# Half of gate_a moved from TensorE to VectorE, with four smaller edits, in a one-core hybrid mLSTM layer step

## The chip, the cores and the metric

The kernel runs on one core of one Trainium2 chip. The metric is device microseconds (us) of one execution, inputs in the chip's main memory at the start and outputs there at the end. Everything is single precision; the large products are done as three matmuls each on rounded parts (high by high, high by low, low by high), written "hi" and "lo" in the code.

## The reference, cut to what matters

```python
mod = silu(c) @ ada_w + ada_b            # (2048) @ (2048, 6*2048), for c_ctx and for c
shift_a, scale_a, gate_a, shift_f, scale_f, gate_f = mod split in 6
h = rmsnorm(x, norm_w[0]) * (1 + scale_a) + shift_a
q, k, v, o, gates, u = split(h @ w_in)   # 1024, 1024, 1024, 1024, 32, 1024 columns
hm = mlstm_bidirectional(q, k, v, gates, states)
hm = rmsnorm(hm) * sigmoid(o)
hp = pool_mixer(u)
mix = concat(hm, hp) @ w_out             # (T, 2048) @ (2048, 2048)
x = x + gate_a * rmsnorm(mix, norm_w[1])
h = rmsnorm(x, norm_w[2]) * (1 + scale_f) + shift_f
y = square(relu(h @ w1)) @ w2            # 2048 -> 8192 -> 2048
x = x + gate_f * rmsnorm(y, norm_w[3])
```

There are 384 tokens: 128 of a context (modulated by `c_ctx`) and 256 latent ones (modulated by `c`); `GROUPS` in the kernel are these two ranges of columns. The outputs are `x` and the final mLSTM states of the context.

## The kernel before, in words

Activations lie transposed, features on the 128 partitions and the 384 tokens along the free axis, in tiles of `[128, 386]` (`slot`). A weight tile of `[128, 1024]` (512 KB) is loaded by the SP queue (`load_w`, L118), rounded to its high part by ScalarE (L124), and its low part is made by VectorE (L125). There are three raw buffers and four of each part. `gemm_T` takes such tiles in order: per tile 24 matmuls (8 times `mm3`, L133 to L135), and after each tile it calls the *feeds*: generators that each advance by `rate` steps a call (`Feed`), so that side work is written between the matmuls of the main work. A scheduler then orders each engine's queue from the order in the program, by its own estimate of what is ready when.

Stages: **u and v** (to about 209 us; eight steps of two 128-row blocks, five weight chunks each, with the matvecs for shift_a and scale_a between them by `ADA_STEPS`), **q and k** (209 to 415 us; four pairs of products; the first takes pooling and gates as feeds, the other three take `attention` of the heads before), **o** (to 502 us), **w_out** (502 to 646 us, 32 weight tiles), then the row norm `r1` (`token_rstd_rows`, L771, POOL at L186, L194) and `make_h2` (L823 to L831), then the **MLP**: per 1024 hidden features four `gemm_T` on w1 (128 x 386 columns: 384 tokens and two columns that carry the shift), and `mlp_out` on w2 (L876 to L878, 128 x 512). From 744 us on this repeats eight times. A tail of norm and residual ends it.

The modulation vectors are matvecs over `ada_w`, 512 KB a load (L212 or L250), four buffers under the tag `ada`. They are made in two ways:

- `ada_mat`, on TensorE: per load four matmuls of 256 columns (L216), which the trace shows as eight records, since a single-precision matmul has two; they lie in four column groups of the array. It ends with a copy (L221) and small matmuls (L224).
- `ada_vec`, on VectorE: per load, products with a per-partition scalar added into an accumulator `ada_acc` (L261 the first, L263 the others), here 512 columns wide, two rows of `ada_w` a load and two conditions, so four instructions a load. It ends with four matmuls by ones (L274), a copy (L276) and small transposing matmuls (L280).

Before the change: shift_a and scale_a by `ada_mat` in the u and v stage; gate_a by `ada_mat` (feed `ada1`, 0.75 steps a call); scale_f and shift_f by `ada_vec` in eight blocks of 512 columns (feed `ada2`, 1.32 steps a call); the first quarter of gate_f by `ada_mat`, the rest by `ada_vec`. Of that first quarter's eight loads four are done while `r1` is worked out (`fill`), four between the first w1 matmuls (`first_side`). gate_a scales the output of w_out as it leaves PSUM (L755).

Of the kernel before, what the change touches and what calls it, by code (L numbers as in the profile page):

```python
# [29 lines left out]
N_E = 1  # L30
ADA_STEPS = (3, 3, 3, 0, 0)
X_ORDER = "tatatatabtatatatat"
N_X = 2


@with_exitstack
def hymba_kernel(
# [26 lines left out]
    cc = const.tile([P, 2, 16], F32, name="cc")  # L64
    prm = const.tile([P, 2, P], F32, name="prm")
# [134 lines left out]

    def ada_mat(parts, tags=("ada",)):


        n, nk = len(parts), parts[0][2]
        w, nj = nk * P, 8 // nk
        ps = bank(f"ada_{parts[0][0]}_{parts[0][1]}")
        for b, (i, k0, _) in enumerate(parts):
            c0 = i * D + k0 * P
            for j0 in range(0, 16, nj):
                tag = tags[b % len(tags)]  # L210
                raw = wp.tile([P, nj, w], F32, tag=tag, name=f"ada_raw_{i}_{k0}_{j0}", bufs=N_W if tag == "lo" else N_ADA)
                nc.sync.dma_start(raw, aw[:, j0:j0 + nj, c0:c0 + w])  # L212
                for a in range(nj):
                    j = j0 + a
                    g = j % 4
                    nc.tensor.matmul(ps[32 * g:32 * g + 32, 0:w], cT[:, j, 6 - 2 * b:38 - 2 * b], raw[:, a, :],  # L216
                                     start=b == 0 and j < 4, stop=b == n - 1 and j >= 12)
# [228 lines left out]
    def gates():  # L446
# [19 lines left out]
        tri = ((C_U, C_NU), (C_L, C_NL))  # L466
        for d in range(2):
            r = slice(32 * d, 32 * d + 8)
            for i in range(3):
                cols = slice(i * P, (i + 1) * P)  # L470
                nc.tensor.matmul(ps_a[r, cols], gv[:, i, d, 0, :], ident, start=True, stop=False)
                nc.tensor.matmul(ps_a[r, cols], lf[:, i, d, :], cst[:, tri[d][1], :], start=False, stop=True)
                nc.tensor.matmul(ps_b[r, cols], lf[:, i, d, :], cst[:, tri[d][0], :], start=True, stop=True)
        for d in range(2):
# [27 lines left out]
        for src, dst in ((aS, acol), (bS, ecol), (gS, gcol)):  # L502
            ps = bank("ps_col")
            i0 = 1 if dst is gcol else 0
            for i in range(i0, 3):
                nc.tensor.matmul(ps[:, i * 40:(i + 1) * 40], src[0:40, i, :], ident[0:40, 0:40], start=True, stop=True)
# [170 lines left out]

# [139 lines left out]
    def make_h2(k):  # L817
# [4 lines left out]
        m = mo[k]  # L822
        nc.vector.tensor_tensor(m[:, 0:NTOK], r1bc[:, 0:NTOK], m[:, 0:NTOK], op=ALU.mult)  # L823
# [245 lines left out]
```

## Time and profile before

| what | value |
|---|---|
| median of 3 runs | 1751.73 us (1749.28 to 1759.74) |
| profiled execution: time, span | 1754.28 us, 1752.6 us |
| busy: TensorE, its weight loads, VectorE, ScalarE, GpSimd | 1716.6, 1537.4, 1065.9, 639.4, 144.3 us |
| mean granted clock of TensorE | 0.996 |
| transfers | 320.74 MB, 183 GB/s over the span |

In the views, PE is TensorE's matmuls, PEld its weight loads, DVE is VectorE, ACT is ScalarE, POOL is GpSimd, and SPq is the SP queue that issues transfers. A matmul is pipelined: its record lasts about 340 ns while the next starts 175 ns later, so what it costs is read from the distance of starts, and not from its duration. `x8` in a row of the timeline is a merged run of eight records.

### The profile page before, as it was taken

How to read it: one execution, taken by the hardware profiler on the slowest of the kernel's cores; microseconds unless marked ns; L12 is line 12 of the kernel's file. 1: busy time of each engine (PE TensorE's matmuls, PEld its weight loads, DVE VectorE, ACT ScalarE, POOL GpSimd, SP SyncE). 2: the span in 40 equal slices, each digit the busy share in tenths (PEclk: the TensorE clock that was granted, in tenths of full speed). 3: DMA queues.
4: the chain of work that ended last, by engine and by line, in shares of the span. 5: the costliest groups of instructions: out<-in, count | busy, mean ns of one | idle time of the engine just before them, and what ended most of it. 6: DMA issues, size and time to landing. Idle time of an engine off the chain costs nothing.

```text
span 1752.6 us, 24767 instructions
## 1 busy us (share of the span) xinstructions
PE 1716.6 (98%) x9617; PEld 1537.4 (88%) x9617; DVE 1065.9 (61%) x1760; ACT 639.4 (36%) x1092; POOL 144.3 (8%) x186
## 2 busy tenths in 40 slices
PE   6999999999999999999999999999999999999997
PEld 3777899998899989988988988988988988998986
DVE  3677658787898849974444843448444444443446
ACT  4322344445433336432332432422332332332332
POOL 0000001111102225430000000000000000000100
PEclk9999999999999999999999999999999999999999
DMA  9888957877777775773434734435444435434543
GB/s 304 276 281 282 304 155 245 250 233 230 237 239 232 237 252 160 201 216 122 129 122 126 219 124 123 130 121 168 130 123 124 129 121 168 131 122 139 170 135 108
DMA packets 249605, 320.74 MB, mean 183 GB/s; under 512 B 14368, under 2 KB 186000, under 8 KB 249104
## 3 DMA queue, kind: packets, MB, share of 16 engines
q1 hardware_dynamic: 242096, 303.61, 55.6%
q0 software_dynamic: 5728, 13.69, 2.8%
q10 hardware_dynamic: 1664, 1.87, 0.3%
q8 instruction: 75, 1.23, 0.3%
q14 instruction: 42, 0.34, 0.1%
HBM read 308.61 MB, written 10.51 MB: 182 GB/s over the span
## 4 chain that ended last, share of the span: by engine, by line
PE 86%; DVE 5%; DMA 5%; issue 2%; POOL 1%; ACT 1%; SPq 1%; ACTq 0%; DVEq 0%; POOLq 0%
PE acc_w L133 10%; PE acc_w L134 10%; PE acc_w L135 10%; PE y L876 10%; PE y L877 10%; PE y L878 10%; DMA ada_raw<-in_ada_w_dram 2%; PE ada L216 2%; DVE ada_acc L263 2%; PE acc_wo L133 1%; PE acc_wo L135 1%; PE acc_wo L134 1%; PE acc_o L133 1%; PE u L390 1%; PE u L389 1%
## 5 line engine op out<-in xcount | busy, mean ns | idle before, releaser
L125 DVE TENSOR_TENSOR lo_w<-raw_w,hi_w 128x1024 fp32r<-128x1024 f32 x256 | 313.9, 1226 | 433.3 <-ACT hi_w L124 433.0
L124 ACT ACTIVATE hi_w<-raw_w 128x1024 fp32r<-128x1024 f32 x256 | 271.5, 1061 | 685.4 <-PE acc_w L134 316.1
L133 PE MATMUL acc_w<-h2h,hi_w 128*128 128x386 f32 x1024 | 347.6, 341 | 2.4 <-ACT h2h L827 2.4
L134 PE MATMUL acc_w<-h2l,hi_w 128*128 128x386 f32 x1024 | 348.3, 340 | 0.0
L135 PE MATMUL acc_w<-h2h,lo_w 128*128 128x386 f32 x1024 | 348.1, 340 | 0.0
L263 DVE SCALAR_TENSOR_TENSOR ada_acc<-ada_raw,sg,ada_acc 128x512 f32<-128x512 f32 x330 | 236.7, 767 | 17.3 <-DMA ada_raw<-in_ada_w_dram 17.3
L133 PEld LDWEIGHTS acc_w<-h2h,hi_w 128*128 128x128 f32 x1024 | 194.5, 190 | 5.0 <-ACT h2h L827 3.0
L134 PEld LDWEIGHTS acc_w<-h2l,hi_w 128*128 128x128 f32 x1024 | 194.2, 190 | 0.8 <-issue 0.4
L135 PEld LDWEIGHTS acc_w<-h2h,lo_w 128*128 128x128 f32 x1024 | 194.0, 189 | 0.1
L216 PE MATMUL ada<-ada_raw,cT 128*32 128x256 f32 x832 | 61.2, 394 | 3.7 <-DMA ada_raw<-in_ada_w_dram 3.6
L900 DVE TENSOR_TENSOR y<-y,y 128x512 f32<-128x512 f32 x81 | 55.9, 692 | 11.7 <-PE y L878 11.3
L124 ACT ACTIVATE hi_wo<-raw_wo 128x1024 fp32r<-128x1024 f32 x32 | 34.1, 1067 | 73.0 <-DMA raw_wo<-in_w_out_dram 43.2
L795 POOL DMA_DIRECT2D gf_dram<-gfT x1 | 0.5, 521 | 698.3 <-DVE gfT L794 698.3
L125 DVE TENSOR_TENSOR lo_wo<-raw_wo,hi_wo 128x1024 fp32r<-128x1024 f32 x32 | 38.8, 1221 | 17.9 <-ACT hi_wo L124 17.9
L389 PE MATMUL v<-hi_v,hh 128*128 128x384 f32 (+1 forms) x144 | 48.5, 337 | 0.0
L867 ACT ACTIVATE z<-z,bz 128x128 f32<-128x128 f32 (+1 forms) x128 | 47.4, 441 | 1.0 <-DVE z L865 0.9
L391 PE MATMUL v<-hi_v,hl 128*128 128x384 f32 (+1 forms) x144 | 46.7, 324 | 0.0
L390 PE MATMUL v<-lo_v,hh 128*128 128x384 f32 (+1 forms) x144 | 46.5, 323 | 0.0
L133 PE MATMUL acc_k<-hh,hi_k 128*128 128x384 f32 x128 | 44.7, 349 | 0.0
L133 PE MATMUL acc_o<-hh,hi_o 128*128 128x384 f32 x128 | 44.6, 348 | 0.0
L133 PE MATMUL acc_q<-hh,hi_q 128*128 128x384 f32 x128 | 44.5, 348 | 0.0
L216 PEld LDWEIGHTS ada<-ada_raw,cT 128*32 128x32 f32 x832 | 19.7, 109 | 27.4 <-issue 14.7
(949 smaller groups left out, 3627.0 us busy)
## 6 DMA issues: line engine op xcount, KB each, us to landing
raw_w<-in_w_dram SPq DMA_DIRECT2D x256, 512.0 KB, 3.7
ada_raw<-in_ada_w_dram SPq DMA_DIRECT2D x192, 512.0 KB, 4.8
raw_wo<-in_w_out_dram SPq DMA_DIRECT2D x32, 512.0 KB, 5.0
raw_u<-in_w_in_dram SPq DMA_DIRECT2D x16, 512.0 KB, 7.5
raw_q<-in_w_in_dram SPq DMA_DIRECT2D x16, 512.0 KB, 5.9
raw_k<-in_w_in_dram SPq DMA_DIRECT2D x16, 512.0 KB, 4.9
raw_o<-in_w_in_dram SPq DMA_DIRECT2D x16, 512.0 KB, 5.0
raw_v<-in_w_in_dram SPq DMA_DIRECT2D x16, 384.0 KB, 7.5
```

What stands on the lines that cost most here:

```text
L124: nc.scalar.activation(hi[:, 0:n], raw[:, 0:n], AF.Copy)
L125: low = lambda: nc.vector.tensor_tensor(lo[:, 0:n], raw[:, 0:n], hi[:, 0:n].bitcast(F32), op=ALU.subtract)
L133: nc.tensor.matmul(ps, lh, rh, start=start, stop=False)
L134: nc.tensor.matmul(ps, lh, rl, start=False, stop=False)
L135: mm3.ins = nc.tensor.matmul(ps, ll, rh, start=False, stop=stop).ins
L216: nc.tensor.matmul(ps[32 * g:32 * g + 32, 0:w], cT[:, j, 6 - 2 * b:38 - 2 * b], raw[:, a, :], start=b == 0 and j < 4, stop=b == n - 1 and ...
L263: nc.vector.scalar_tensor_tensor(acc[:, g, :], raw[:, a, :], cj, acc[:, g, :], op0=ALU.mult, op1=ALU.add)
L389: nc.tensor.matmul(acc[i][:, 0:n], xh[:, sl], hi[:, k, :], start=k == 0, stop=False)
L390: nc.tensor.matmul(acc[i][:, 0:n], xh[:, sl], lo[:, k, :], start=False, stop=False)
L876: nc.tensor.matmul(acc, xh[:, s], hi, start=k == 8 * ch, stop=False)
L877: nc.tensor.matmul(acc, xh[:, s], lo, start=False, stop=False)
L878: nc.tensor.matmul(acc, xl[:, s], hi, start=False, stop=k == 8 * ch + 7)
```

## The change

- gate_a: of its 16 blocks of 128 columns the last eight stay with `ada_mat` (feed `ada1`, now at 0.35 steps a call); the first eight go to `ada_vec`.
- `ada_vec` for scale_f, shift_f and that half of gate_a runs in five blocks of 1024 columns (one row of `ada_w` a load, so two instructions of 1024 columns), at 1.5 steps a call in q and k and 1.3 in o and w_out. `prm` moves from the pool `const` to the pool `pre`.
- gate_a is applied in `make_h2` (a fused scale and multiply per token group, in place of one multiply), and the copy out of PSUM becomes plain.
- All eight `ada_mat` loads of gate_f come in two calls of `fill`, the second behind the broadcast of `r1`; its second four loads go to the still unused output tiles `y[0]`, `y[1]`.
- After the first MLP chunk's w2 product has begun, `norm_h2` multiplies h2 by the second row norm and adds the shift, so that all later w1 products have 384 columns and leave PSUM by `evac_normed`.
- In `gates` the matmuls of the two directions alternate; eight small matmuls by the identity (L506) become transposes.
- `ADA_STEPS` goes from (3, 3, 3, 0, 0) to (4, 0, 4, 1, 0).

```diff
-ADA_STEPS = (3, 3, 3, 0, 0)
+ADA_STEPS = (4, 0, 4, 1, 0)
+RATES = (1.5, 1.3, 1.3)
+RATE_MAT = 0.35
...
-                raw = wp.tile([P, nj, w], F32, tag=tag, ...)
+                if raws and tag is None:
+                    raw = raws.pop(0).rearrange("p (j c) -> p j c", c=w)
+                else:
+                    raw = wp.tile([P, nj, w], F32, tag=tag, ...)
...
-        for d in range(2):
-            r = slice(32 * d, 32 * d + 8)
-            for i in range(3):
-                ...
+        for i in range(3):
+            for part in range(3):
+                for d in range(2):
+                    r = slice(32 * d, 32 * d + 8)
+                    ...
-                nc.tensor.matmul(ps[:, i * 40:(i + 1) * 40], src[0:40, i, :], ident[0:40, 0:40], start=True, stop=True)
+                nc.tensor.transpose(ps[:, i * 40:(i + 1) * 40], src[0:40, i, :], ident[0:40, 0:40])
...
-        for i in (4, 3):
-            for q in range(4):
-                yield from ada_vec(i, 512 * q, 512, att)
-    ada1 = Feed(mid_mat(), 0.75)
-    ada2 = Feed(mid_vec(), 1.32)
+        for i, q in ((4, 0), (4, 1), (3, 0), (3, 1), (2, 0)):
+            yield from ada_vec(i, 1024 * q, 1024, att)
+    ada1 = Feed(ada_mat([(2, 8 + 2 * b, 2) for b in range(4)]), RATE_MAT)
+    ada2 = Feed(mid_vec(), RATES[0])
...
-            for g, (a, b) in enumerate(GROUPS):
-                nc.scalar.activation(m[:, a:b], mo[u][:, a:b], AF.Copy, scale=mod[:, 2, u, g:g + 1])
+            nc.scalar.activation(m[:, 0:NTOK], mo[u][:, 0:NTOK], AF.Copy)
...
+    def norm_h2():
+        for k, (hi, lo) in enumerate(h2):
+            t = mlp.tile([P, NTOK], F32, tag="z", name=f"h2n{k}")
+            nc.vector.tensor_tensor(t, hi[:, 0:NTOK].bitcast(F32), lo[:, 0:NTOK].bitcast(F32), op=ALU.add)
+            nc.vector.tensor_tensor(t, t, r2bc, op=ALU.mult)
+            for g, (a, b) in enumerate(GROUPS):
+                sh = mod[:, 3, k, g:g + 1]
+                nc.scalar.activation(hi[:, a:b], t[:, a:b], AF.Identity, bias=sh)
+                nc.vector.scalar_tensor_tensor(lo[:, a:b], t[:, a:b], sh, hi[:, a:b].bitcast(F32), op0=ALU.add, op1=ALU.subtract)
+            yield
+    def evac_normed(t, ps):
+        z = mlp.tile([P, NTOK], F32, tag="z", name=f"z{t}")
+        nc.scalar.activation(z, ps[:, 0:NTOK], AF.Relu)
+        nc.vector.tensor_tensor(z, z, z, op=ALU.mult)
+        hid[t] = split_T(z, f"hid{t}")
...
-        yield from ada_mat([(5, 0, 2), (5, 2, 2)])
+        yield from ada_mat([(5, 0, 2), (5, 2, 2)], ("ada", None), [y[i][:, 1024 * n:1024 * n + 1024] for i in range(2) for n in range(2)])
...
         r1bc = token_rstd_rows([sqa, sqs[0], sqs[1]], "r1", fill)
+        fill()
...
-        nc.vector.tensor_tensor(m[:, 0:NTOK], r1bc[:, 0:NTOK], m[:, 0:NTOK], op=ALU.mult)
+        for g, (a, b) in enumerate(GROUPS):
+            nc.vector.scalar_tensor_tensor(m[:, a:b], m[:, a:b], mod[:, 2, k, g:g + 1], r1bc[:, a:b], op0=ALU.mult, op1=ALU.mult)
...
+        elif ch < 7:
+            gemm_T(w1, [grp(4 * ch + 4)], hx2, NTOK, evac_normed, (ff, fx), name="w1")
...
+        ws = mlp_out(ch, (ff, fx, fn) if ch == 0 else (ff, fx), done if ch == 7 else None)
+        if ch == 0:
+            fn.finish()
```

In `first_side` three of the four steps of gate_f that stood between the w1 matmuls go, since `fill` has taken the loads.

More of the change, by code (lines that the diff above doesn't have):

```diff
@@ L64, in hymba_kernel @@
     cc = const.tile([P, 2, 16], F32, name="cc")
-    prm = const.tile([P, 2, P], F32, name="prm")
+    vp_scope, pre_scope = ExitStack(), ExitStack()
+    vp = vp_scope.enter_context(tc.tile_pool(name="vp", bufs=1))
+    pre = pre_scope.enter_context(tc.tile_pool(name="pre", bufs=1))
+    prm = pre.tile([P, 2, P], F32, name="prm")
     nc.sync.dma_start(cc[:, 0, :], c_ctx.rearrange("(p j) -> p j", j=16))
@@ L68, in hymba_kernel @@
     nc.sync.dma_start(cst[:, 0:3], cs_src[:, 0:3])
-    vp_scope, pre_scope = ExitStack(), ExitStack()
-    vp = vp_scope.enter_context(tc.tile_pool(name="vp", bufs=1))
     vsb = [vp.tile([P, NH, 129], F32, name=f"v{i}") for i in range(3)]
     gsb = vp.tile([P, 3, 32], F32, name="gsb")
-    pre = pre_scope.enter_context(tc.tile_pool(name="pre", bufs=1))
     x_tok = [pre.tile([P, D], F32, tag=f"x{i}", name=f"xtok{i}") for i in range(3)]
@@ L199, in hymba_kernel, with ada_mat @@
     aw = ada_w.rearrange("(p j) n -> p j n", j=16)
-    def ada_mat(parts, tags=("ada",)):
+    def ada_mat(parts, tags=("ada",), raws=None):
         n, nk = len(parts), parts[0][2]
@@ L210, in ada_mat @@
                 tag = tags[b % len(tags)]
-                raw = wp.tile([P, nj, w], F32, tag=tag, name=f"ada_raw_{i}_{k0}_{j0}", bufs=N_W if tag == "lo" else N_ADA)
+                if raws and tag is None:
+                    raw = raws.pop(0).rearrange("p (j c) -> p j c", c=w)
+                else:
+                    raw = wp.tile([P, nj, w], F32, tag=tag, name=f"ada_raw_{i}_{k0}_{j0}", bufs=N_W if tag == "lo" else N_ADA)
                 nc.sync.dma_start(raw, aw[:, j0:j0 + nj, c0:c0 + w])
@@ L466, in gates @@
         tri = ((C_U, C_NU), (C_L, C_NL))
-        for d in range(2):
-            r = slice(32 * d, 32 * d + 8)
-            for i in range(3):
[L470 to L473, printed above, removed]
+        for i in range(3):
+            cols = slice(i * P, (i + 1) * P)
+            for part in range(3):
+                for d in range(2):
+                    r = slice(32 * d, 32 * d + 8)
+                    if part == 0:
+                        nc.tensor.matmul(ps_a[r, cols], gv[:, i, d, 0, :], ident, start=True, stop=False)
+                    elif part == 1:
+                        nc.tensor.matmul(ps_a[r, cols], lf[:, i, d, :], cst[:, tri[d][1], :], start=False, stop=True)
+                    else:
+                        nc.tensor.matmul(ps_b[r, cols], lf[:, i, d, :], cst[:, tri[d][0], :], start=True, stop=True)
         for d in range(2):
@@ L664, in attention @@
         yield
-    def mid_mat():
-        for hb in range(2):
-            yield from ada_mat([(2, 8 * hb + 2 * b, 2) for b in range(4)])
     def mid_vec():
-        for i in (4, 3):
-            for q in range(4):
-                yield from ada_vec(i, 512 * q, 512, att)
-    ada1 = Feed(mid_mat(), 0.75)
-    ada2 = Feed(mid_vec(), 1.32)
+        for i, q in ((4, 0), (4, 1), (3, 0), (3, 1), (2, 0)):
+            yield from ada_vec(i, 1024 * q, 1024, att)
+    ada1 = Feed(ada_mat([(2, 8 + 2 * b, 2) for b in range(4)]), RATE_MAT)
+    ada2 = Feed(mid_vec(), RATES[0])
     def qk(g, feeds):
@@ L700, in hymba_kernel @@
         fa.finish()
+    ada2.rate = RATES[1]
     mixs = [None] * KT
@@ L732, in hymba_kernel @@
         mixs[k] = split_T(mix[k][:, 0:NTOK], f"mx{k}")
+    ada2.rate = RATES[2]
     mo = [None] * KT
@@ L785, in hymba_kernel @@
     gf_dram = dram.tile([32, P], F32, name="gf_dram")
+    def norm_h2():
[13 more added lines that the diff above has]
+        hid[t] = split_T(z, f"hid{t}")
+    y = [mlp.tile([P, D], F32, name=f"y{i}", bufs=1) for i in range(3)]
     def gate_f():
-        yield from ada_mat([(5, 0, 2), (5, 2, 2)])
+        yield from ada_mat([(5, 0, 2), (5, 2, 2)], ("ada", None), [y[i][:, 1024 * n:1024 * n + 1024] for i in range(2) for n in range(2)])
         for q in (1, 2, 3):
@@ L869, in evac_hid @@
         hid[t] = split_T(z, f"hid{t}")
-    y = [mlp.tile([P, D], F32, name=f"y{i}", bufs=1) for i in range(3)]
     w2v = wview(w2)
@@ L908, in first_side @@
         for n in range(3):
-            with tc.issue_after(mm3.ins):
-                next(gfg)
+            if n == 0:
+                with tc.issue_after(mm3.ins):
+                    next(gfg)
             yield
@@ L915, in first_side @@
             yield
-        with tc.issue_after(mm3.ins):
-            next(gfg)
         for k in range(12, 16):
@@ L931, in gate_late @@
             yield
-    fx, ff = Feed(first_side(), 1.0), Feed(gate_late(), 0.2)
+    fx, ff, fn = Feed(first_side(), 1.0), Feed(gate_late(), 0.2), Feed(norm_h2(), 1.0)
     gemm_T(w1, [grp(0), grp(1), grp(2)], hx2, 386, evac_hid, (fx,), name="w1", hold=lambda ki, g: make_h2.ins if ki == 1 and g == 0 else ())
@@ L1003, in hymba_kernel @@
     for ch in range(8):
-        if ch < 7:
-            gemm_T(w1, [grp(4 * ch + 4)], hx2, 386, evac_hid, (ff, fx), name="w1")
+        if ch == 0:
+            gemm_T(w1, [grp(4)], hx2, 386, evac_hid, (ff, fx), name="w1")
+        elif ch < 7:
+            gemm_T(w1, [grp(4 * ch + 4)], hx2, NTOK, evac_normed, (ff, fx), name="w1")
         if ch == 6:
@@ L1009, in hymba_kernel @@
             load_tail()
-        ws = mlp_out(ch, (ff, fx), done if ch == 7 else None)
+        ws = mlp_out(ch, (ff, fx, fn) if ch == 0 else (ff, fx), done if ch == 7 else None)
+        if ch == 0:
+            fn.finish()
         if ch < 7:
             for g in range(1, 4):
-                gemm_T(w1, [grp(4 * ch + 4 + g)], hx2, 386, evac_hid, (ff,), name="w1")
+                gemm_T(w1, [grp(4 * ch + 4 + g)], hx2, NTOK, evac_normed, (ff,), name="w1")
     with tc.manual_schedule(engines={mybir.EngineType.DVE}):
```

## The prediction

> **What bounds the kernel now.** I read the busy shares first, then the chain that ended last, then busy time by stage.
>
> ```profile
> PE 1716.6 (98%) x9617; PEld 1537.4 (88%) x9617; DVE 1065.9 (61%) x1760; ACT 639.4 (36%) x1092; POOL 144.3 (8%) x186
> PE 86%; DVE 5%; DMA 5%; issue 2%; POOL 1%; ACT 1%; SPq 1%; ACTq 0%; DVEq 0%; POOLq 0%
> 270.00:420.00 150.00, 147.97 (x1008) 136.73 (x1011) 117.64 (x257) 73.47 (x209) 24.23 (x27) 1.00 0.78 245
> 420.00:502.00 82.00, 81.42 (x537) 74.28 (x530) 73.96 (x148) 36.44 (x89) 6.25 (x7) 1.00 0.75 235
> 502.00:646.00 144.00, 142.06 (x825) 139.01 (x823) 113.45 (x152) 54.21 (x91) 32.67 (x30) 0.99 0.76 235
> 653.00:744.00 91.00, 90.76 (x519) 87.83 (x520) 82.71 (x158) 49.76 (x105) 42.97 (x53) 0.98 0.63 183
> ```
>
> In the window rows the columns after the length are PE, PEld, DVE, ACT and POOL with counts, then clock and DMA share. TensorE sets the time in every stage (the chain is 86% its own work), so an instruction taken off it counts almost in full. VectorE is the second: 78% in q and k, 90% in o, 79% in w_out, 91% at the start of the MLP. What is moved there has little room. So I price TensorE's gains first, and then ask whether VectorE keeps up.
>
> **The change part by part.**
>
> **gate_a.** The price of a matvec load on TensorE is read from its neighbours:
>
> ```profile
> 458.07 0.34 PE L135 MATMUL acc_o<-hh,lo_o 128*128 128x384 f32 x1
> 458.34 0.64 PE L216 MATMUL ada<-ada_raw,cT 128*32 128x256 f32 x8
> 458.91 0.44 PE L133 MATMUL acc_o<-hh,hi_o 128*128 128x384 f32 x1
> 459.19 0.34 PE L134 MATMUL acc_o<-hl,hi_o 128*128 128x384 f32 x1
> L274 PE MATMUL adav<-ada_acc,cst 128*32 128x256 f32 x88 | 7.0, 389 | 0.0
> L280 PE MATMUL adaf<-cst,adav_sb 128*128 128x4 f32 x44 | 5.8, 237 | 1.9 <-ACT adav_sb L276 1.9
> ```
>
> From 458.07 to 459.19 are 1.12 us for two steps of the main stream, which alone take 0.35 (0.175 each, below); the load costs 0.77. Four blocks of 256 columns of gate_a leave, four loads each: 16 x 0.77 = 12.3 us. One closing pair of L224 goes too; I price its four records like four of L280, 5.8 / 44 x 4 = 0.5. Against this stand the closings of `ada_vec`: eight of 7.0 / 11 + 5.8 / 11 = 1.17 are 9.4 us now; five with double columns and double small matmuls cost between 5.9 (no dearer) and 11.7 (twice). I take 11.0, nearest to twice, since the columns stream: +1.6. Sum -11.2 (bounds -16.3 and -10.5).
>
> **gate_f.** Four loads move from the w1 stream to the wait behind the broadcast of `r1`:
>
> ```profile
> 647.83 1.93 PE L216 MATMUL ada<-ada_raw,cT 128*32 128x256 f32 x32
> 653.24 2.30 PE L133 MATMUL acc_w<-h2h,hi_w 128*128 128x386 f32 x6 [2.41 <-ACT h2h L827]
> 652.00:656.00 4.00, 2.76 (x9) 2.77 (x10) 4.00 (x13) 2.41 (x9) 0.00 (x0) 0.63 1.05 344
> 660.82 0.57 PE ada L216 x8
> 699.82 0.57 PE ada L216 x8
> ```
>
> The first and the last of the four that go are the last two rows: 4 x 0.77 = -3.1. In their new place TensorE idles 2.41 us for h2, and four loads last 1.93 (the row of x32), so they fit. The cover is the landing of those loads: SP must issue them into `y[0]`, `y[1]`, that is once the tiles of attention there are free (the last reader is the last L274, near the end of w_out), ahead of SP's w1 weights and beside POOL's 16 loads of `xTr`. At 644 to 648 the DMA share is already full:
>
> ```profile
> 628.00:632.00 4.00, 4.00 (x25) 4.00 (x24) 0.17 (x1) 3.07 (x7) 2.55 (x4) 1.00 0.42 122
> 644.00:648.00 4.00, 4.00 (x34) 3.97 (x36) 0.06 (x1) 2.32 (x7) 0.00 (x0) 1.00 1.04 367
> ```
>
> 2.1 MB at 367 GB/s are 5.7 us, and half of 628 to 632 is free; I cost it at 0, and up to +3 if they land late, since PE is in order and w1 stands behind them. The clock fell after that idle time (0.63 from 652 to 656): about 3.4 us at half speed, worth up to 1.7. I count -0.5 of it, since h2's pace limits the same stretch. [...]
>
> **gate_a in `make_h2`.** One multiply becomes two fused ones:
>
> ```profile
> L823 DVE TENSOR_TENSOR mo<-tr_r,mo 128x384 f32<-128x384 f32 x16 | 8.5, 549 | 1.0 <-PE tr_r L194 1.0
> L828 DVE SCALAR_TENSOR_TENSOR h2l<-mo,mod,h2h 128x256 fp32r<-128x256 f32 x16 | 9.2, 575 | 0.0
> L828 DVE SCALAR_TENSOR_TENSOR h2l<-mo,mod,h2h 128x128 fp32r<-128x128 f32 x16 | 6.8, 424 | 0.0
> ```
>
> 424 + 575 - 549 = 0.45 us more per tile, 7.2 in all, in a stage where VectorE idles 91 - 82.7 = 8.3. The first tile is on the path (+0.4); for the pace I add +0.5 (0 to +4). The new wait, `make_h2` on the end of gate_a's matvec, comes under VectorE below. The plain copy on ScalarE (37% in w_out) is worth nothing.
>
> **w1 with 384 columns.** Undisturbed stretches, first and last row of each, 384 and 156 matmuls:
>
> ```profile
> 811.65 0.34 PE L133 MATMUL acc_w<-h2h,hi_w 128*128 128x386 f32 x1
> 879.49 0.34 PE L135 MATMUL acc_w<-h2h,lo_w 128*128 128x386 f32 x1
> 592.06 0.34 PE L133 MATMUL acc_wo<-mx6h,hi_wo 128*128 128x384 f32 x1
> 619.23 0.34 PE L135 MATMUL acc_wo<-mx15h,lo_wo 128*128 128x384 f32 x1
> ```
>
> 67.84 / 383 = 0.1771 and 27.17 / 155 = 0.1753: 0.0018 each. 27 of the 32 column groups have 96 such matmuls: 2592 x 0.0018 = -4.7. By the share of columns alone (2 / 386 of 0.1771) it would be -2.4. I take the measured row. [...]
>
> `norm_h2` pays for it with 16 x (2 x 0.549 + 0.424 + 0.575) = 33.6 us of VectorE while w2 of the first chunk runs:
>
> ```profile
> 744.00:778.00 34.00, 34.00 (x151) 27.58 (x150) 29.41 (x48) 10.87 (x14) 14.36 (x24) 1.00 0.82 240
> 778.00:811.00 33.00, 33.00 (x144) 26.67 (x143) 13.50 (x14) 8.48 (x8) 0.00 (x0) 1.00 0.40 127
> ```
>
> 42.9 + 33.6 = 76.5 in 67 us; but 11.9 of the 42.9 are gate_f's L263, needed by the very end only and free to slide behind 811. That leaves 64.6: it fits, cost 0, and +9 if nothing slides, since the weights' low parts queue behind.
>
> **gates.** 36 records of 18 matmuls alternate in one column group, one each 0.108 us (218.48 to 222.08 with the first row after them). Where the two directions met by chance, they ran in pairs:
>
> ```profile
> 218.48 0.39 PE L471 MATMUL ps_a<-cst,gsb 128*8 128x128 f32 x2
> 220.12 0.27 PE L472 MATMUL ps_a<-cst,lf 128*8 128x128 f32 x1
> 220.13 0.27 PE L471 MATMUL ps_a<-cst,gsb 128*8 128x128 f32 x1
> 222.08 0.45 PE L133 MATMUL poolo<-p00h,hi_pw 128*128 128x384 f32 x1
> 229.41 1.91 PE ps_col L506 x16
> 315.12 0.66 PE hT L661 x6
> ```
>
> 0.01 apart: all in pairs saves 1.5 of the 3.6. The transposes (L661: 0.11 each, one record) take 8 x 0.11 for 1.91: -1.0. Sum -2.5 (bounds -2.9, 0).
>
> **ADA_STEPS.** Three loads in one run cost less than three alone:
>
> ```profile
> 105.39 1.50 PE L216 MATMUL ada<-ada_raw,cT 128*32 128x256 f32 x24
> 117.10 0.64 PE L216 MATMUL ada<-ada_raw,cT 128*32 128x256 f32 x8 [0.49 <-DMA ada_raw<-in_ada_w_dram]
> ```
>
> Runs of 1, 3 and 4 loads take 0.64, 1.50 and 1.93: each run has some 0.25 us of its own. The eight loads of a step now fall into runs of 3, 3, 1 and 1; two runs of 4 save 2 x 0.25, and the lone load's DMA wait of 0.49 may go or grow, since a run of four wants all four `ada` buffers at once. Seven steps: -2.5, between -5 and +7 (a wait of 1 us more a step).
>
> **Does VectorE keep up?** 64 loads of four 512-column instructions become 80 loads of two 1024-column ones.
>
> ```profile
> L263 DVE SCALAR_TENSOR_TENSOR ada_acc<-ada_raw,sg,ada_acc 128x512 f32<-128x512 f32 x330 | 236.7, 767 | 17.3 <-DMA ada_raw<-in_ada_w_dram 17.3
> L125 DVE TENSOR_TENSOR lo_w<-raw_w,hi_w 128x1024 fp32r<-128x1024 f32 x256 | 313.9, 1226 | 433.3 <-ACT hi_w L124 433.0
> L900 DVE TENSOR_TENSOR y<-y,y 128x512 f32<-128x512 f32 x81 | 55.9, 692 | 11.7 <-PE y L878 11.3
> 549.65 0.50 PE L280 MATMUL adaf<-cst,adav_sb 128*128 128x4 f32 x3 [1.94 <-ACT adav_sb L276]
> ```
>
> L263 at 1024 isn't shown: between 0.767 (no dearer) and 1.53 (twice). L125 and L900 show 512 more columns of a two-input operation at 0.534, so 1.30. Then 160 x 1.30 = 208 against 256 x 0.767 = 196: +12 us, spread over q, k, o and w_out, where VectorE idles 71 of 376 us, TensorE's saving taking 11 of them. It fits on average. But an attention step or a weight's low part now waits behind 1.3 us instead of 0.77, o stands at 90%, and one stall of this kind is there already: 1.94 us at 547, with the clock's fall some 3.7 in all. I add +2 (-3.7 to +10).
>
> **Sum**: -11.2 - 3.1 - 0.5 + 0.4 + 0.5 - 4.7 - 2.5 - 2.5 + 2 = -21.6 us. Against the profiled execution (span 1752.6, time 1754.28) that is 1732.7. The median, 1751.73, lies 2.6 below it; the forecast is 1730.
>
> **The rivals.** *VectorE or attention swallows half* (0.13): of the loads taken from q, k and o the time comes back as waits for VectorE's queue. For: 90% in o. Against: TensorE idled only 2.6 us in 270 to 502. +10: 1740.
> *The u and v stage waits for its loads* (0.07): the bound of +7 instead of -2.5: 1740.
> *All runs smoother* (0.20): the stall at 547 goes (-5.7 against my +2), the clock holds (-1.2), runs of four work (-2.5): 1721.
> *Slower* (0.05): the last `ada_vec` block, gate_a's own, now ends where `make_h2` needs it. A block of 1024 has 19 steps, one of 512 had 11: 95 steps, less 24 x 1.5 in q and k and 16 x 1.3 in o, leave 38.2, at 1.3 due by call 30 of the 32 of w_out; now 88 steps at 1.32 end at call 67 - 40 = 27. VectorE idled 30 us in w_out; 10 go by the later end. If a 1024-column instruction costs 1.7 (twice 0.767, and a tenth for POOL's traffic), 160 x 0.40 = 64 us overrun 20 of slack by 44, and all of w1 waits: 1730 + 44 = 1774. It decides from about 1.56 (42 us) on. L125 speaks against it.
>
> **How the numbers follow.** The forecast has 0.55, most of it within 1722 to 1738. A measurement tells about 1% here (17.5 us, 1734.2). Faster by over 1%: 0.55 x 0.9 + 0.20 = 0.70; within 1%: the rest of the forecast, both rivals at 1740 and part of the last, 0.27; slower 0.03. The range is 1714 to 1746: below it lies the end of the smoother case with all lower bounds, above it two upper bounds at once or the slow rival, under 0.2 together.
>
> **What would show it.** In the profile after: L216 with 128 records fewer (704) and none behind 653 us; L263 at 1024 columns near 1.30; w1 from the second chunk at 0.1753 a matmul; a row of x32 or two at the start of w1, no idle 2.4 before it, the clock at 1.00 there; the start of w1 some 14 us earlier than 653.24 (-11.2 - 2.5 - 2.5 + 2 + 0.4); DVE over 85% in q and k. Wrong would be: idle rows of PE with DVE as releaser in q to w_out, `make_h2` waiting for L280, L216 waiting for loads in the first 200 us or at the start of w1.

## The result, and the profile after

| | before | after |
|---|---|---|
| median of 10 runs each | 1750.55 us (1748.08 to 1759.74) | 1740.88 us (1739.47 to 1745.21) |
| ratio of after to before, 95% interval | | 0.9939 (0.9926 to 0.9951) |
| profiled execution, span | 1752.6 us | 1739.2 us |

The change makes the kernel 0.6% faster. The sign is as forecast and the time lies inside the range (1714 to 1746 us), but less than half of the forecast gain came, and the outcome held most likely, faster by over 1% (0.70), did not. From the page of after, its busy shares and the chain that ended last:

```profile
PE 1695.3 (97%) x9461; PEld 1528.6 (88%) x9461; DVE 1084.5 (62%) x1620; ACT 630.4 (36%) x1050; POOL 150.5 (9%) x186
PE 77%; DVE 9%; DMA 6%; issue 6%; POOL 1%; ACT 1%; SPq 0%; DVEq 0%; POOLq 0%; ACTq 0%
```

TensorE lost 21.3 us of busy time (the prediction's terms for its own work add up to 24.0), but the span fell by 13.4. The chain hints at the rest: TensorE's own work was 86% of it and is 77%, VectorE's share went from 5% to 9%, and that of "issue", time for which the profile shows no wait, from 2% to 6%. The stages, from the start of the first matmul of each to that of the next ("q and k with attention" starts with attention's first matmul, `mb`), beside the prediction's terms put to the stage in which they fall (us):

| stage | before | after | change | predicted | terms |
|---|---|---|---|---|---|
| u, v | 208.7 | 204.4 | -4.3 | -2.5 | ADA_STEPS |
| first q and k | 62.5 | 57.8 | -4.7 | -4.8 | gates -2.5, three loads of gate_a -2.3 |
| q and k with attention | 143.5 | 146.3 | +2.8 | | |
| o | 87.9 | 89.5 | +1.6 | | |
| w_out | 143.2 | 141.8 | -1.4 | | |
| these three | 374.6 | 377.6 | +3.0 | -6.9 | the rest of gate_a -8.9, VectorE +2 |
| `r1`, first w1 products | 98.4 | 96.8 | -1.6 | -2.7 | gate_f -3.1, clock -0.5, h2 +0.9 |
| MLP | 998.7 | 992.9 | -5.8 | -4.7 | 384 columns |
| tail | 9.6 | 9.7 | +0.1 | 0 | |

So the miss is in one place: 10 us between the first attention and the end of w_out. (The -4.3 of u and v is in part luck: ten kernels here have this order of loads, and 204.4 is the shortest of them, see `e12_both_steps`.) The windows of after for these stages (columns as in the prediction) and TensorE's waits in 204 to 640 us, with total, count and longest:

```profile
262.25:408.52 146.27, 137.25 (x894) 129.51 (x893) 124.41 (x214) 70.60 (x201) 29.76 (x27) 0.99 0.74 231
408.52:498.00 89.48, 86.05 (x538) 80.22 (x534) 73.11 (x108) 41.38 (x96) 7.61 (x7) 0.98 0.70 225
498.00:639.79 141.79, 140.89 (x818) 137.98 (x815) 126.13 (x124) 49.67 (x75) 33.24 (x30) 1.00 0.82 262
```

```profile
PE hT L670 <- DVE hs L635: 7.1, 4, 2.3
PE inter L623 <- ACT num L633: 5.3, 4, 2.3
PE ps_col L515 <- issue: 1.0, 1, 1.0
PE acc_wo L137 <- DVE lo_wo L127: 0.9, 2, 0.8
```

Before, the same list read:

```profile
PE inter L614 <- ACT num L624: 2.4, 5, 0.7
PE adaf L280 <- ACT adav_sb L276: 1.9, 1, 1.9
PE hT L661 <- DVE hs L626: 0.2, 1, 0.2
```

VectorE has room on the average of each stage (85%, 82% and 89% busy), and still TensorE stands 12.4 us at two lines of the attention where it stood 2.6. The timeline of after shows one of these stops, on VectorE, GpSimd and TensorE:

```profile
354.05 1.28 DVE L268 SCALAR_TENSOR_TENSOR ada_acc<-ada_raw,sg,ada_acc 128x1024 f32<-128x1024 f32 x1
355.25 0.16 DVE L187 TENSOR_SCALAR rsh<-ssh 128x2 f32<-128x2 f32 x1
355.32 1.28 DVE L268 SCALAR_TENSOR_TENSOR ada_acc<-ada_raw,sg,ada_acc 128x1024 f32<-128x1024 f32 x1
357.18 0.42 DVE L635 TENSOR_TENSOR hs<-hs,rsh 128x256 f32<-128x256 f32 x1 [0.58 <-POOL rsh L188]
```

```profile
355.49 1.66 POOL L188 TENSOR_TENSOR rsh<-rsh,mhalf 128x2 f32<-128x2 f32 x1 [8.13 <-DVE rsh L187]
...
345.13 0.61 PE L623 MATMUL inter<-C,q 128*128 128x129 f32 x4
...
357.66 0.69 PE L670 MATMUL hT<-cst,hs 128*128 128x128 f32 x2 [2.28 <-DVE hs L635]
...
358.79 0.52 PE L137 MATMUL acc_q<-hh,lo_q 128*128 128x384 f32 x1
359.11 0.52 PE L135 MATMUL acc_q<-hh,hi_q 128*128 128x384 f32 x1
```

From the last `inter` (345.13) a chain of some ten short steps of ScalarE, VectorE and GpSimd leads to `hs`, which the transposes hT take. In before no `ada_vec` operation lay among them in VectorE's queue in the same attention:

```profile
353.76 0.71 PE L614 MATMUL inter<-C,q 128*128 128x129 f32 x4 [0.37 <-ACT num L624]
...
363.92 0.82 PE L661 MATMUL hT<-cst,hs 128*128 128x128 f32 x6
361.45 0.43 DVE L626 TENSOR_TENSOR hs<-hs,rsh 128x256 f32<-128x256 f32 x1 [0.81 <-POOL rsh L186]
```

There `hs` was ready 8.1 us after the last `inter`, and hT was due 10.2 us after it, 48 main matmuls later: 2 us of slack. The first three attentions of before were alike (8.1 to 8.2 us); the fourth had seven `ada_vec` operations of 512 columns on its chain, took 11.0 us, and TensorE stood 0.2 us at its hT: the sign that the slack was nearly used was there. In after six operations of 1.28 us lie between the steps shown (the first at 345.50, the last at 355.32), and `hs` is ready after 12.5 us. And behind the stop the matmuls start 0.32 us apart (358.79 to 359.11) and not 0.175: the clock fell to half for 3.4 us. For each such fall that is a loss of 1.7 us by the clock, an estimate from its share of 0.50; by these starts it is 1.5. After has two (from 357.6 and from 408.8 us).

### The profile page after: what moved, and what is told of

It reads as the page before. It is cut to its first block, busy times and chain, and to the rows that moved or that the text cites. A ratio compares the mean times of both kernels' runs of the same rounds, so it can differ in the third digit from the quotient of the medians.

```text
span 1739.2 us, 24241 instructions
## 1 busy us (share of the span) xinstructions
PE 1695.3 (97%) x9461; PEld 1528.6 (88%) x9461; DVE 1084.5 (62%) x1620; ACT 630.4 (36%) x1050; POOL 150.5 (9%) x186
## 4 chain that ended last, share of the span: by engine, by line
PE 77%; DVE 9%; DMA 6%; issue 6%; POOL 1%; ACT 1%; SPq 0%; DVEq 0%; POOLq 0%; ACTq 0%
PE y L901 10%; PE y L902 10%; PE y L903 10%; PE acc_w L136 9%; PE acc_w L137 9%; PE acc_w L135 9%; DVE ada_acc L268 4%; PE ada L221 2%; DMA raw_u<-in_w_in_dram 1%; DMA raw_v<-in_w_in_dram 1%; PE acc_q L135 1%; PE acc_o L135 1%; PE acc_q L136 1%; PE acc_q L137 1%; PE acc_o L137 1%
## 5 line engine op out<-in xcount | busy, mean ns | idle before, releaser
L136 PE MATMUL acc_w<-h2l,hi_w 128*128 128x384 f32 (+1 forms) x1024 | 346.2, 338 | 0.5 <-DVE h2l L857 0.5
L137 PE MATMUL acc_w<-h2h,lo_w 128*128 128x384 f32 (+1 forms) x1024 | 345.5, 337 | 0.0
L135 PE MATMUL acc_w<-h2h,hi_w 128*128 128x384 f32 (+1 forms) x1024 | 343.7, 337 | 0.7 <-ACT h2h L853 0.6
L268 DVE SCALAR_TENSOR_TENSOR ada_acc<-ada_raw,sg,ada_acc 128x1024 f32<-128x1024 f32 (+1 forms) x240 | 257.2, 1108 | 2.8 <-DMA ada_raw<-in_ada_w_dram 2.7
L806 DVE TENSOR_TENSOR z<-z 128x384 f32<-128x384 f32 x54 | 30.0, 556 | 53.6 <-ACT z L805 53.4
L925 DVE TENSOR_TENSOR y<-y,y 128x512 f32<-128x512 f32 x81 | 55.6, 691 | 11.3 <-PE y L903 10.9
L805 ACT ACTIVATE z<-acc_w 128x384 f32<-128x384 f32 x54 | 26.3, 488 | 75.7 <-PE acc_w L137 75.7
L221 PE MATMUL ada<-ada_raw,cT 128*32 128x256 f32 x672 | 46.0, 395 | 1.1 <-DMA ada_raw<-in_ada_w_dram 1.1
```

The source lines that it names most:

```text
L135: nc.tensor.matmul(ps, lh, rh, start=start, stop=False)
L136: nc.tensor.matmul(ps, lh, rl, start=False, stop=False)
L137: mm3.ins = nc.tensor.matmul(ps, ll, rh, start=False, stop=stop).ins
L268: nc.vector.scalar_tensor_tensor(acc[:, g, :], raw[:, a, :], cj, acc[:, g, :], op0=ALU.mult, op1=ALU.add)
L925: nc.vector.tensor_tensor(dst, acc[i], dst, op=ALU.add)
```

## The experiments

"Chain" is the time from the last `inter` to `hs` ready, for the four attentions; "place" is when hT is due, had it not to wait.

**The four other edits alone** (`e1_four`): gate_a stays on TensorE and is applied on the way out of PSUM, at the old rates; scale_f and shift_f run in 512 columns again. The lines for these last two are:

```diff
-        for i, q in ((4, 0), (4, 1), (3, 0), (3, 1), (2, 0)):
-            yield from ada_vec(i, 1024 * q, 1024, att)
+        for i in (4, 3):
+            for q in range(4):
+                yield from ada_vec(i, 512 * q, 512, att)
...
```

> The four merged edits alone: gate_a wholly on TensorE at 0.75 steps a call and applied on the way out of PSUM, scale_f and shift_f in 512-column instructions at 1.32, all else as after the change. By stages of the two profiles the four gave -4.2 us in u and v, -1.6 at the start of w1, -5.8 in the MLP and perhaps -2.5 in gates. All theories: 1737 to 1739, no idle at the attention matmuls beyond the 2.6 us of before. That would make the move of gate_a a loss of 2 to 4 us. If instead it lies above 1743, gate_a's move did pay and the loss lies elsewhere.

Measured: 1745.76 us (1739.02 to 1747.98), ratio 0.9959 (0.9944 to 0.9974), -7.2 us. The MLP took 992.3 us (-6.4, predicted -4.7), and the first q and k 60.3 (-2.2, predicted -2.5 for the gates). Idle in q to o was 1.3 us. The 1737 to 1739 that all theories gave did not come: TensorE stood still elsewhere, in 160 to 720 us:

```profile
PE tr_r L196 <- DVE dg_r L194: 3.9, 2, 3.8
PE u L394 <- ACT hh L358: 3.6, 2, 3.5
PE adaf L285 <- ACT adav_sb L281: 2.0, 1, 2.0
```

Three stops of 2 to 4 us, each with a fall of the clock (the mean of this profile is 0.993, before it was 0.996), eat some of the gain. By the text above, a time over 1743 means that gate_a's move did pay: on top of these four edits it is worth some 3.5 us (0.9939 against 0.9959, with intervals that just overlap).

**Half of gate_a off TensorE and on nobody** (`e2_half_out`): the first half of gate_a is not computed (set to 0), `ada_vec` as before in blocks of 512.

> As the changed kernel, but with 512-column instructions at 1.32 steps a call for scale_f and shift_f alone; the first half of gate_a is left out of the computation (set to zero). TensorE has the 16 loads less and VectorE nothing more. Width theory (attention's short VectorE steps wait behind 1.28 us instructions) and amount theory (VectorE has too much to do): the 11 us come in full, 11 below the four edits alone, about 1727. Filler theory (TensorE's matvec loads only filled the time in which it would have waited for attention, whose own chain sets q and k): no more than 3 us below the four edits alone, about 1736, with idle rows at the attention matmuls.

Measured: 1733.77 us (1728.06 to 1737.35), ratio 0.9893 (0.9876 to 0.9910), 12 us below the kernel with the four edits. The loads are worth about what the prediction said (-11.2) when VectorE doesn't take them over; chain 6.9, 8.2, 8.8, 11.3 us.

**The whole change in 512-column operations** (`e3_narrow`), with rates 1.74, 1.5, 1.5 for the same work by the same time:

> The whole change with ten blocks of 512 columns instead of five of 1024, at 1.74, 1.5, 1.5 steps a call (same share of the work per call). Width theory: the idle at attention falls from 12.4 us to about 3 and both falls of the clock go: 1730, though VectorE has 30 us more to do. Amount theory: more idle than after the change, 1745 or more. Filler theory: 1741, the same idle.

Measured: 1771.46 us, ratio 1.0102 (1.0086 to 1.0118). The width theory's 1730 is far off, but its mechanism shows: no wait at hT is left (chain 9.1, 8.3, 11.2, 10.8 us), and q and k with attention take 4.0 us less than in after. What costs more is behind them: the same work in narrow operations keeps VectorE busy 23 us longer (1107.6 against 1084.5), in w_out it was busy for 96% of the window below, the weights' low parts came late, and so did all that stands behind w_out:

```profile
498.00:640.00 142.00, 134.86 (x786) 129.24 (x785) 136.11 (x195) 47.02 (x70) 28.66 (x12) 1.00 0.74 236
```

```profile
PE tr_r L776 <- ACT sq_mo L756: 10.2, 1, 10.2
PE acc_wo L137 <- DVE lo_wo L127: 6.1, 7, 2.0
```

```profile
669.60 1.06 ACT L126 ACTIVATE hi_w<-raw_w 128x1024 fp32r<-128x1024 f32 x1 [14.59 <-DMA raw_w<-in_w_dram]
```

The 10.2 us are a risk that the prediction had named under gate_f: gate_f's loads into `y` went out at 647.6 us (627.0 in after), a w1 weight behind them landed only at 669.6, and in ScalarE's queue its rounding stands ahead of the last squares, `sq_mo`.

**The four edits and 1024-column operations, gate_a on TensorE** (`e4_four_wide`), rate 1.14:

> The four edits alone, with scale_f and shift_f in four blocks of 1024 columns at 1.14 steps a call; gate_a wholly on TensorE. Width theory: idle at attention appears although no work was moved, 5 to 10 us above the four edits alone, about 1745. Amount theory: a little below the four edits alone, since VectorE has 30 us less to do. Filler theory: equal to the four edits alone within 2 us.

Measured: 1744.55 us, ratio 0.9958 (0.9946 to 0.9971), as the kernel with the four edits. Against that kernel's profile, wide operations cost 3.3 us in q and k and 3.6 in o, and gained 4.8 in w_out. The chain took 11.4, 6.6, 11.6 and 6.1 us, with four, no, four and no operations of 1024 columns on it: what counts here is not how much VectorE does in the stage but whether loads fall between the steps of this chain.

**The power without GpSimd** (`e5_nopow`): the square root is left out.

```diff
-            rstd_cols(rsh[:, i, h0:h0 + 2], ssh[:, i, h0:h0 + 2], 2, 1.0 / P)
+            r = rsh[:, i, h0:h0 + 2]
+            nc.vector.tensor_scalar(r, ssh[:, i, h0:h0 + 2], 1.0 / P, EPS, op0=ALU.mult, op1=ALU.add)
+            nc.vector.reciprocal(r, r)
```

> The changed kernel, with the power that GpSimd computes for the attention's normalisation (12 operations of 128x2) replaced by two operations of the vector engine, a multiply-add and a reciprocal; the square root is left out, so the scale is 1/x instead of 1/sqrt(x) (same amount of work behind it). Theory 'GpSimd held': the stops of TensorE at hT (7.1 us of idle in q..w_out) come from the power, which takes 1.67 us beside a 1024-wide operation and 0.7 us alone, and from its two hand-overs; then the idle at hT falls below 3 us, the two falls of the clock near 356 and 407 us go with it (1.7 us each), and the kernel takes 1732 to 1736 us. Rival 'a queue of long operations': each short step of the attention waits behind a 1.28 us operation of the vector engine whoever computes the power; then hT keeps 5 us or more and the time stays between 1739 and 1742 us.

Measured: 1732.45 us, ratio 0.9892 (0.9875 to 0.9910), the idle at hT 0.7 us. That is the number of the theory, but not its proof. The chain became only 1.2 us shorter on average (12.0, 10.6, 9.1, 11.5), since the two new steps now queue on VectorE. The scheduler, for its part, had put the last two transposes 8 matmuls (1.4 us) further back in two of the four attentions. How much of the gain is GpSimd's and how much the place's, this run cannot tell; the runs below move the place alone.

**The old places of the loads in u and v** (`e6_steps`):

```diff
-ADA_STEPS = (4, 0, 4, 1, 0)
+ADA_STEPS = (3, 3, 3, 0, 0)
```

> The changed kernel with the loads of u and v placed as before, (3, 3, 3, 0, 0) in place of (4, 0, 4, 1, 0). Theory of the prediction (the new places save 2.5 us): 1743 to 1744 us, u and v 2 to 3 us longer than 204.4 us. Rival 'the places are worth nothing, and the last load ahead of the closing steps costs a wait of 1.9 us for h': 1738 to 1740 us, with no idle of TensorE at the last step of u. Rival 'the 4.3 us that u and v gained come from the places': 1745 us.

Measured: 1743.40 us (1739.68 to 1743.94), ratio 0.9953 (0.9936 to 0.9970), which overlaps with after. Its u and v took 206.2 us in the profile. See the pair at the end for the verdict.

**gate_a's part alone on the kernel before** (`e7_gate_only`):

> The kernel before with only the gate_a part of the change: half of gate_a's matvec on the vector engine, 1024-column operations, rates 1.5, 1.3, 1.3, gate_a used in the residual; the four other changes are left out. Theory 'parts add': the whole gave -10.7 us and the four alone -7.2 us by their ratios, so this gives -3 to -4 us, about 1747 us, with TensorE idle 10 to 14 us in q to w_out and a w_out some 2 us shorter. Rival 'gate_a is worth its predicted 9 us (11.2 less 2) and the four lose it again': 1741 to 1743 us. Rival 'the attention takes all of it': 1750 to 1755 us.

Measured: 1752.93 us (1748.71 to 1756.05, 12 runs), ratio 1.0004 (0.9993 to 1.0016): no change, as the last of the three theories had it. The waits of its profile are those of after:

```profile
PE hT L661 <- DVE hs L626: 6.8, 4, 2.1
PE inter L614 <- ACT num L624: 4.3, 4, 2.3
```

So on the kernel before, the part that names the change gave back all it took from TensorE, and most of the whole's gain is that of the other edits (-7.2 of -10.7 by the ratios). That the two parts add up to some 4 us less than the whole is left open: the profiled execution of this kernel took 1749.17 us, 3.8 less than its median, so its trace doesn't show where the others were longer.

**The loads moved from the attention to w_out** (`e8_rates`):

```diff
-RATES = (1.5, 1.3, 1.3)
+RATES = (1.2, 1.3, 1.45)
```

> The changed kernel with the vector engine's loads spread otherwise: rate 1.2 in place of 1.5 beside the attention in q and k (29 steps in place of 36), 1.3 in o as it is, 1.45 in place of 1.3 in w_out. Theory 'the attention's short steps pay for each long operation beside them': q and k fall by 3 to 5 us from 146.3 us, the idle at hT and inter from 12.4 to below 9 us, w_out grows by at most 2 us: 1736 to 1739 us. Rival 'any load at all does it, the amount does not matter': 1740 to 1742 us with the idle unchanged. Rival 'the last block comes late': the idle after w_out grows from 1.7 us to 5 us or more, 1744 to 1750 us.

Measured: 1759.24 us, ratio 1.0042 (1.0026 to 1.0059). Both halves of the theory hold, with the wrong size for the second: q and k fell by 2.2 us and o by 5.6 (chain 11.7, 5.1, 12.1, 5.1), and w_out grew by 16.5. VectorE's window and TensorE's waits there:

```profile
498.00:640.00 142.00, 135.40 (x765) 130.90 (x764) 135.02 (x128) 47.36 (x69) 35.22 (x24) 0.99 0.79 251
```

```profile
PE acc_wo L137 <- DVE lo_wo L127: 6.6, 6, 2.3
PE adaf L285 <- ACT adav_sb L281: 6.4, 2, 6.1
```

With VectorE busy for 95% of this window instead of 89%, the weights' low parts are late, and the last block ends behind w_out (6.1 us, with the clock at half from 651.6 to 665.2; the mean of the whole profile is 0.989). Over the whole stage, longer by these waits, the share is 88% (138.7 of 158.3 us), no higher than in after: the share alone doesn't tell the two apart. The third theory, 1744 to 1750, has this mechanism at too low a price. Between rates 1.3 and 1.45 the room in w_out runs out.

**hT 24 matmuls later** (`e9_late`): the last step of each attention goes into the next group.

```diff
+    late = ()
     for g in range(1, 4):
         fa = Feed(attention(g - 1), 1.0)
-        qk(g, (fa, ada1, ada2))
-        fa.finish()
+        qk(g, (*late, fa, ada1, ada2))
+        late = (fa,)
...
-            fa.finish()
+            late = (fa,)
```

> The changed kernel with the last step of each attention (the six transposes hT of hs and what follows) moved behind the first 24 matmuls of the next group, 4.2 us later at 0.175 us each; the loads and the vector engine's work are the same. Theory 'the chain of hs ends 2 us too late for its place in TensorE's queue': the idle at hT (7.1 us) goes, with the falls of the clock behind it (2 x 1.7 us): 1731 to 1735 us. Rival 'TensorE is bound by the vector engine in these stages whatever its order': the idle comes back at another place (inter, lo_q, lo_k) and the time stays between 1738 and 1742 us.

Measured: 1736.79 us (1732.59 to 1739.75), ratio 0.9908 (0.9888 to 0.9929). The wait at hT is gone though the chain is as long (12.0, 12.2, 9.5, 11.4), since its place is 13.8 us or more after `inter`. 4.8 us at `inter` stay, with two falls of the clock behind them (the mean of this profile is 0.995), so the time lies between the two expectations. The trace beside the stop shown above:

```profile
347.72 0.61 PE L623 MATMUL inter<-C,q 128*128 128x129 f32 x4
...
361.56 0.82 PE L671 MATMUL hT<-cst,hs 128*128 128x128 f32 x6
```

**The squares out of the PSUM bank** (`e10_scratch`):

```diff
-                nc.scalar.activation(ps[:, 260:388], hs[:, hl, :], AF.Square, accum_out=...)
+                nc.scalar.activation(num[:, 0, 0:128], hs[:, hl, :], AF.Square, accum_out=...)
```

> The changed kernel, in which the squares of hs, of which only the sum is used, are written over the numerator in SBUF and no longer into the PSUM bank of the numerator; the bank then comes free after the addition of intra (L626) and not after the square (L633), some 6 us later in the trace. Theory 'inter waits for that bank': the 5.3 us of idle at inter go, 1735 to 1737 us. Rival 'inter's wait hides the lateness of what follows': hT waits longer by as much, 1739 to 1742 us.

Measured: 1743.41 us (1741.45 to 1745.33), ratio 0.9946 (0.9926 to 0.9965): the rival, a little above its 1742. What `inter` no longer waits (2.6 us left), hT waits more:

```profile
PE hT L670 <- DVE hs L635: 9.4, 4, 3.4
PE inter L623 <- ACT num L633: 2.6, 2, 1.3
```

**Both** (`e11_both`), and **both with the old ADA_STEPS** (`e12_both_steps`):

> The changed kernel with both edits: hT 24 matmuls later, and the squares in SBUF. If the two stops are independent: idle in q to o falls from 13.4 to below 2 us and the time to 1727 to 1731 us. If the vector engine is what holds these stages (85% and 82% busy): above 1735 us.

> As the kernel before this one, with the loads of u and v at their old places, (3, 3, 3, 0, 0). By the prediction's term the new places save 2.5 us, so this would be 2 to 3 us slower than with them. Rival 'the last u step waits for a weight load that the eight new places delay': no idle at the last step of u, no fall of the clock there (in most profiles of the new places there is one), and a time 1 to 3 us shorter than with the new places.

Measured: 1731.12 us (1728.76 to 1735.46), ratio 0.9882 (0.9862 to 0.9901), and 1731.74 us (1730.58 to 1735.99), ratio 0.9885 (0.9866 to 0.9904). These beat both kernels, after by some 10 us. The amount of work is after's; the place of attention's last step and the tile that takes the squares have changed. The first one's profile (span 1728.6, clock 0.999), by its own stages (q and k with attention, o):

```profile
264.00:403.17 139.17, 135.36 (x888) 127.38 (x887) 122.76 (x212) 69.88 (x201) 30.19 (x26) 1.00 0.75 237
403.17:488.82 85.65, 85.07 (x544) 79.37 (x540) 73.85 (x111) 40.80 (x94) 8.28 (x8) 1.00 0.75 246
```

VectorE does the same work as in after in less time (122.8 us of 139.2 against 124.4 of 146.3, and 73.9 of 85.7 against 73.1 of 89.5), so it was not its capacity that held these stages. q, k, o and w_out take 139.2 + 85.6 + 141.5 = 366.3 us, 8.3 less than before, where the prediction had 6.9 less. The idle time in q to o, with the first stage's 1.0 at ps_col, is 5.4 us, above the 2 that were expected, and the time 0.1 above the 1731.

The pair shows no difference for ADA_STEPS: 0.6 us apart, with intervals that overlap, where one theory had 2 to 3 us more and the other 1 to 3 less. Over all profiles u and v took 204.4 to 211.7 us with the new places (ten kernels, median 209.6) and 206.2 to 208.7 with the old ones (four). With the new places each of the ten has an idle time of 1.9 to 4.5 us at the last step of u, with the old ones none has. ScalarE shows why, here in the kernel without GpSimd's power:

```profile
190.00 0.84 ACT L126 ACTIVATE hi_v<-raw_v 128x768 fp32r<-128x768 f32 x1 [2.83 <-DMA raw_v<-in_w_in_dram]
190.75 1.48 ACT L358 ACTIVATE hh<-hm,mod 128x128 fp32r<-128x128 f32 x4
```

```profile
191.19 0.80 PE L394 MATMUL u<-hi_u,hh 128*128 128x512 f32 x1 [4.06 <-ACT hh L358]
```

In ScalarE's queue `hh`, which TensorE wants, stands behind the rounding of a weight that has not landed.

## Why the prediction was right or wrong

- **The step that failed is "Does VectorE keep up?"**, +2 us with an upper bound of +10. In after the idle time at hT and `inter` is 12.4 us against 2.6, and two falls of the clock add 3.4 by the clock's share, while the stall at 547 us (1.9 us with its fall of 1.7) is gone but for 0.75: 9.8 + 3.4 - 1.2 - 1.7 = +10.3, just past the bound. Against the +2 in the sum that is 8.3 of the 9.9 us by which these stages missed; where the other 1.6 went is not shown. The mechanism was named (an attention step waits behind 1.3 us), and the rival "VectorE or attention swallows half" with its 1740 is what happened. Its size was judged by the average room in a stage. It is decided by one chain: ten steps, 8.1 us long, due after 10.2, whose squares also free the bank that `inter` waits for. The rows of before that show both times were there to read; in the attention shown, six operations of 1.28 us on that chain are 7.7 us, of which 4.4 lengthened it, against a slack of 2. That moving hT's place and that bank alone brings 9.8 us back shows the cause.
- **The argument against that rival** ("TensorE idled only 2.6 us") shows that the chain was in time, not by how much.
- **gate_a on TensorE**: -11.2, about right; the kernel without the work was 12 below the one with the four edits, and the first q and k lost 4.7 with 4.8 predicted, gates included. The five wide closings took 1.06 us each for the products with ones and, estimated as eight of 52 records that took 6.4 us together, 0.98 for the small matmuls: 10.2 in all, where 11.0 were priced.
- **L263 at 1024 columns**, 1.30 us, right, and so 704 L216 records (L221 in after; 672 and 32 on the tiles `y`):

```profile
L268 DVE SCALAR_TENSOR_TENSOR ada_acc<-ada_raw,sg,ada_acc 128x1024 f32<-128x1024 f32 x150 | 194.7, 1325 | 2.8 <-DMA ada_raw<-in_ada_w_dram 2.7
L221 PE MATMUL ada<-ada_raw,cT 128*32 128x256 f32 x672 | 46.0, 395 | 1.1 <-DMA ada_raw<-in_ada_w_dram 1.1
L279 PE MATMUL adav<-ada_acc,cst 128*32 128x512 f32 x40 | 5.3, 605 | 0.0
L285 PE MATMUL adaf<-cst,adav_sb 128*128 128x4 f32 x52 | 6.4, 243 | 0.0
```

  Of the 150, 114 ran with no GpSimd operation beside them and took 1.28 us on average; 12 ran beside its additions of squares (`sqa`, L748) and took 1.78. Before, at 512 columns, the same means were 0.75 (266 operations) and 1.19 (12).

- **384 columns**: -5.8 against -4.7. First and last row of a stretch of 384 matmuls after:

```profile
803.64 0.34 PE L135 MATMUL acc_w<-h2h,hi_w 128*128 128x384 f32 x1
...
870.63 0.34 PE L137 MATMUL acc_w<-h2h,lo_w 128*128 128x384 f32 x1
```

  66.99 / 383 = 0.1749, so 0.0022 a matmul and not 0.0018: 2592 x 0.0022 = 5.7. `norm_h2` cost nothing.
- **gate_f**: the loads went where they should, and fit, with 0.20 us of waiting for a transfer:

```profile
644.71 1.50 PE L221 MATMUL ada<-y,cT 128*32 128x256 f32 x24
646.42 0.64 PE L221 MATMUL ada<-y,cT 128*32 128x256 f32 x8 [0.20 <-DMA y<-in_ada_w_dram]
647.17 0.97 PE L135 MATMUL acc_w<-h2h,hi_w 128*128 128x386 f32 x4
```

  `r1` to w1 takes 7.4 us as before, the clock stays at 1.00 (before, it was 0.63 from 652 to 656 us); the gain is 1.6 and not 2.7. w1 starts 6.1 us earlier, where 14 were predicted: mostly the miss of q to w_out.
- **ADA_STEPS**: -2.5 is not borne out (above); the 4.3 that u and v lost in after's profile did not come again in nine other kernels. The wait that the bound of +7 stood for did come, in ScalarE's queue and once, not seven times in TensorE's.
- **The median**: I took 2.7 us off (1732.7 to 1730) for the profiled execution of before. After's profiled execution stands at its median, so that is the rest of the miss: (21.6 - 13.4) + 2.7 = 10.9 = 1740.9 - 1730. That the time falls on the rival's 1740 is thus partly luck: q to w_out came 9.9 worse than forecast, `r1` 1.1 worse, u and v 1.8 and the MLP 1.1 better, and the 2.7 come on top.
- **Slower**, the last block late, did not happen, but it was near: with rate 1.45 in w_out the block ended 6.1 us behind it and the kernel took 1759 us.

## What to carry to other kernels

When side work goes to an engine with room on average, look for the chain of short steps on that engine that another engine waits for: its length, the time at which its end is due, and the number of long operations that can stand between its steps decided here (8.1 us, due after 10.2, six operations of 1.28), and not the busy share (85%, 82% and 89% in these stages), as long as the engine wasn't full (in w_out, at the higher rate, there was no room left). When such a chain is late, move the place where its result is taken before taking work away; here 24 matmuls and a PSUM bank were worth what the whole change had been worth.

## What the runs showed of the hardware that I had not expected

GpSimd's power on 2 columns took 0.69 us when VectorE was quiet, 1.12 to 1.14 when it started beside an `ada_vec` operation of 512 columns (four of twelve before) and 1.66 to 1.69 beside one of 1024 (six of twelve in after); the first two from before, and the third is the row at 355.49 above, which ends 0.5 us after VectorE's operation of 355.32:

```profile
360.72 0.69 POOL L186 TENSOR_TENSOR rsh<-rsh,mhalf 128x2 f32<-128x2 f32 x1 [3.10 <-DVE rsh L185]
347.50 1.13 POOL L186 TENSOR_TENSOR rsh<-rsh,mhalf 128x2 f32<-128x2 f32 x1 [1.43 <-DVE rsh L185]
```

In each of these ten GpSimd's operation ended 0.5 to 0.6 us behind VectorE's, and VectorE's own took 0.75 and 1.28 us, as without the power beside it. The other fourteen took 0.69 to 0.73.

In after the clock's fall depended on when a stop came, and not only on its length: a stop of 1.90 us at 407.36 was followed by 3.4 us at half speed, one of 2.28 us at 296.43 and one of 2.13 at 461.06 were not.

```profile
407.36 0.66 PE L670 MATMUL hT<-cst,hs 128*128 128x128 f32 x4 [1.90 <-DVE hs L635]
296.43 0.71 PE L623 MATMUL inter<-C,q 128*128 128x129 f32 x4 [2.28 <-ACT num L633]
461.06 0.44 PE L670 MATMUL hT<-cst,hs 128*128 128x128 f32 x2 [2.13 <-DVE hs L635]
```

In before and in after the falls lie on a grid: in after they start at 357.55 and 408.75 us, 51.20 or 15 times 3.413 apart, in before at 550.67 and 653.07, 102.40 or 30 times, and each lasts 3.41. The stop at 461.06 is cut by a line of after's grid, at 459.95, into 1.0 and 1.1 us. By the windows of these two grids, from 30 us to the tail, both with 2.0 us or more of gaps between TensorE's records (2.4 in before, 2.2 in after) were followed by half speed, of the three with 1.5 to 2.0 us two (1.94 in before and 1.90 in after were, 1.97 in after was not), of the six with 1.0 to 1.5 us none. So the gaps alone do not decide; two windows of after, the first followed by full speed and the second by half:

```profile
292.70:296.11 3.41, 1.44 (x13) 1.25 (x11) 3.41 (x10) 1.90 (x5) 0.00 (x0) 1.00 0.47 176
405.34:408.75 3.41, 1.51 (x15) 0.81 (x14) 1.16 (x3) 0.79 (x1) 0.69 (x1) 1.00 1.01 335
```
